# Decoder layer on one core: block sums of the down projections' weights accumulated in SBUF instead of in DRAM

## The chip, the cores and the metric

The kernel runs on one core of a Trainium2 chip. The metric is the device time of one execution in microseconds (us). TensorE (PE) does the matmuls, with its weight loads (PEld) beside them; VectorE (DVE), ScalarE (ACT) and GpSimd (POOL) work on vectors; SyncE (SP) issues most of the transfers. DMAs that GpSimd issues are on the profile's queue q0 (software_dynamic), those that SyncE issues on q1 (hardware_dynamic); both are served by the core's 16 DMA engines. A DMA that adds to its destination (`accum_op`) is issued by GpSimd here.

## The reference

One layer of a hybrid decoder on 512 tokens of width 1024, in float32:

```
def swiglu(x, w_gate, w_up, w_down):
    return (jax.nn.silu(x @ w_gate) * (x @ w_up)) @ w_down
...
        h = swiglu(rms_norm(x, ffn1_pre_norm[l]), ffn1_w_gate[l], ffn1_w_up[l], ffn1_w_down[l])
        x = x + 0.5 * rms_norm(h, ffn1_post_norm[l])
        ... # sparse attention, gated delta rule, attention to a memory of 256 rows; x = x + their gated sum
        ... # a second swiglu layer (ffn2) of the same form
```

The hidden width of both swiglu layers is 2816, that is 22 tiles of 128. The change is in the two products `@ w_down` (2816 x 1024).

## The kernel before

**Float32 as three matmuls.** Every operand x is split into hi (a cast to fp32r by ACT) and lo = x - hi (a subtraction on DVE). A product is hi\*hi + lo\*hi + hi\*lo, three matmuls. A weight tile of 128x512 (256 KB, here one *piece*) so needs a DMA into a raw tile, a cast, and a subtraction, before PE can use it.

**Seven products for eight.** Both the gate/up products (`fast_phase`) and the down projections (`down7`) use a Strassen-Winograd scheme: 2x2 blocks, seven block products of sums of blocks. In `down7` the blocks of the weights are b00, b01, b10, b11 (an index for the half of the columns, one for the half of the 22 k-tiles). Of H (the hidden activations) DVE makes the sums in SBUF (`s3`, `s2`, `s4`). Each of the seven products m0 to m6 has 11 k-tiles, two blocks of tokens and three matmuls, 66 matmuls of 128x512. The accumulators X, Y, Z, Q are pairs of PSUM banks (acc_mm, acc_e, acc_s, and acc_o with acc_r); `end...` moves or adds them into c2 (SBUF) between products. After m4 (`done(4)`) half of the tokens are complete; m5 and m6 complete the other half.

**Where the weight sums come from.** `weight_sums` writes four sums T into DRAM: t3 = b11+b01, t1 = b01+b00, t2 = t3+b00, t4 = t2+b10. It does so with DMAs on GpSimd's queue, copies first and accumulates on top (line L536). FFN1's 88 pieces of 256 KB go out during FFN1's own gate/up phase, one for each 4600 columns of matmuls (`tick`); FFN2's 32 pieces of 704 KB go out during the mixers, one for each 15000 columns. In `down7` a ring (`ringr` for raw tiles, `ringh` for hi, `lor`/`lo` for lo) then takes the pieces in pairs: load L639 on SP, cast L640, subtraction L641. Some products' tiles go through `wload` (raw tiles `wraw`, L105, L106, L109) instead.

**Around it.** The gate/up phase (f from 6 to 21) loads four quarters of 256 KB a tile f into `fq` (L413 to L416, on SP), DVE adds them into `fs` and back into `fq` (L412), ACT casts them into `fset`/`fxth` (L418, L425), DVE subtracts (L421, L426), PE multiplies (L446), ACT evicts (L452 to L461). During the down projections other transfers run too: the residual `x` (tiles xa, xb; four of 512 KB), the post gain `gb` (512 KB), and in FFN1 the memory rows `xm` (1 MB). In FFN1 the memory's norm and transposes (`mem_norm`, L208 to L213) stand between matmuls of the down projection. A tile scheduler fixes the order of instructions on each engine at build time; an instruction waits for its operands by semaphore, in that order.

Of the kernel before, what the change touches and what calls it, by code (L numbers as in the profile page):

```python
# [39 lines left out]
class Body:  # L40
    def __init__(self, ctx, tc, a, out, tap):
# [28 lines left out]
        self.own = 0  # L70
        self.side = []

# [48 lines left out]
    def tick(self, ins, cols):  # L121

        self.mmark = ins
        if self.side:
            self.cols += cols
            if self.cols >= self.pace:
                self.cols -= self.pace
                self.side.pop(0)()

# [303 lines left out]

    def fast_prods(self, S, T, banks, s7, mid=()):

        nc, v, te = self.nc, self.nc.vector, self.nc.tensor
        hi, lo = S
        a, q7, g, u = banks
        a, q7, u = a[:, :256], q7[:, :256], u[:, :256]

        def prod(out, w, t, start=False):
            th, tl = T[t]
            for k in range(4):
                c = slice(k * P, k * P + P)
                wh, wl = hi[:, w, c], lo[:, w, c]
                m = lambda x, y, **kw: te.matmul(out, x, y, skip_group_check=True, **kw)  # L446
                m(wh, th[:, k], start=start and k == 0, stop=False)
                m(wl, th[:, k], start=False, stop=False)
                self.tick(m(wh, tl[:, k], start=False, stop=k == 3), 3 * 256)
# [7 lines left out]
        nc.scalar.activation(u, a, AF.Copy, scale=-1.0)  # L457
# [66 lines left out]

    def weight_sums(self, w, n, cuts, pace):

        g = self.nc.gpsimd
        nh = self.a[w].shape[1] // 2
        T = [self.dr.tile([nh, P, 512], F32, name=f"T{n}{i}") for i in range(4)]
        v = lambda x: x.rearrange("k p n -> (k p n)").rearrange("(r c) -> r c", c=1024)  # L530
        B = lambda i, j: v(self.a[w][j, nh * i : nh * i + nh])
        t1, t2, t3, t4 = map(v, T)
        todo = ((t3, B(1, 1), 0), (t1, B(0, 1), 0), (t3, B(0, 1), 1), (t1, B(0, 0), 1), (t2, t3, 0), (t2, B(0, 0), 1), (t4, t2, 0), (t4, B(1, 0), 1))

        def piece(o, x, add, c):
            i = g.dma_start(o[c], x[c], max_dma_last_dim=2048, **({"accum_op": OP.add} if add else {}))  # L536
            self.order(i, self.mmark, mybir.DependencyClass.Sync)

        r = nh * P * 512 // 1024 // cuts
        self.pace, self.cols = pace, 0  # L540
        self.side = [lambda s=s, c=slice(r * j, r * j + r): piece(*s, c) for s in todo for j in range(cuts)]
        return T

    def down7_homes(self, n, x1, lors):
# [4 lines left out]
        self.sraw = [dw.tile([P, 4, 256], F32, name=f"sraw{i}") for i in range(2)]  # L549
        self.q7 = dw.tile([P, 2, 512], F32, name="q7")  # L550
        self.c2 = dw.tile([P, 2, 2, 512], F32, name="c2")
        lor = [dw.tile([P, 2, 512], F32R, name=f"lor{i}") for i in range(lors)]
        self.wx = None
        if lors < 4:
            self.wx = pool("wy")
            self.own = 6
        dv = pool("dv")
# [4 lines left out]
        dv = pool("dz")  # L562
        sl0, sl1, sh0, sh1 = (ch(x) for x in ("sl0", "sl1", "sh0", "sh1"))
        self.sring = [sh0, sh1, sh2, sh3], [sl0, sl1, sl2, sl3]
        return gb, lor
# [4 lines left out]

    def down7_ring(self, los):
        rings = [self.cp.tile([P, KT, SEQ], t, tag=g, name=n) for t, g, n in ((F32, "xth", "ringr"), (F32R, "xtl", "ringh"))]
        two = lambda x: [x[:, i : i + 2] for i in range(0, x.shape[1], 2)]
        self.wring = two(rings[0]), two(rings[1]), los

    def down7(self, H, w, T, banks, done, ringed, lor=()):

        nc, v = self.nc, self.nc.vector
        X, Y, Z, Q = banks
        sh, sl = self.sring  # L580
        sraw, q7, c2 = self.sraw, self.q7, self.c2
# [3 lines left out]
        tt, st = v.tensor_tensor, v.scalar_tensor_tensor  # L585

        def s3(k, n):
            t = sraw[slot % 2][:, :n]
            self.order(tt(t, h(0, 0, k, n), h(1, 0, k, n), op=OP.subtract), last)
            return t  # L590

        def s2(k, n):
            a, q = h(0, 0, k, n), h(1, 0, k, n)
            tt(q, h(1, 1, k, n), q, op=OP.subtract)
            st(a, a, -1.0, q, op0=OP.mult, op1=OP.subtract)
            return a

# [7 lines left out]

        def end7(i):
            nc.scalar.copy(q7[:, i], Q[i])

        def end6(i):
            nc.scalar.copy(Z[i], X[i])  # L610

        def end5(i):
            tt(c2[:, 1, i], Z[i], q7[:, i], op=OP.add)

        def end4(i):
            tt(c2[:, 0, i], X[i], q7[:, i], op=OP.add)

        part = lambda i, j: lambda k, n: h(i, j, k, n)
        seq = (
            (X, d[0, :nh], part(0, 0), True, end1, 0),  # L620
            (Q, T[2], s3, True, end7, 0),
            (X, T[1], s2, False, end6, 2),
            (Z, T[0], part(1, 0), False, end5, 0),
            (X, T[3], part(1, 1), False, end4, 0),
            (Y, d[0, nh:], part(0, 1), False, None, 0),
            (Z, d[1, nh:], s4, False, None, 4),
        )
        slot = wslot = 0
        last = None
        wr, wh_, wl_ = self.wring  # L630

        def weights(m, src, ks, lo):
            nonlocal wslot
            if not ringed(m, ks[0]):
                return {ks[0]: self.wload(src[ks[0]], lo=lo)}
            n, k = len(ks), ks[0]
            raw, hi, lo = wr[wslot % len(wr)][:, :n], wh_[wslot % len(wh_)][:, :n], wl_[wslot % len(wl_)][:, :n]
            wslot += 1
            nc.sync.dma_start(raw, src[k : k + n].rearrange("k p n -> p k n"))  # L639
            nc.scalar.copy(hi, raw)  # L640
            tt(lo, raw, hi.bitcast(F32), op=OP.subtract)  # L641
            return {k + i: (hi[:, i], lo[:, i]) for i in range(n)}

        for m, (acc, src, make, start, end, lag) in enumerate(seq):
            ops, ws, groups, k = {}, {}, [], 0
            while k < nh:
                n = 2 if ringed(m, k) and (nh - k) % 2 == 0 else 1
# [3 lines left out]
            lo = list(lor) if lag and not ringed(m, nh - 1) else []  # L651
            hold = len(groups) - lag
# [697 lines left out]
    def run(self):  # L1350
# [3 lines left out]
        with tc.tile_pool(name="f1", bufs=1) as fp, contextlib.ExitStack() as x1:  # L1354
# [41 lines left out]
            with tc.tile_pool(name="wx0", bufs=1) as self.wx:  # L1396
# [16 lines left out]
            with tc.tile_pool(name="st1", bufs=1) as st, tc.tile_pool(name="su1", bufs=1) as su:  # L1413
# [4 lines left out]
                self.fast_phase(1, 4, xh, xl, RB, H, step)  # L1418
                assert not self.side
            gb, lor = self.down7_homes(1, x1, 3)  # L1420
# [33 lines left out]
            uh = ul = None  # L1454
            self.down7(H, "ffn1_d", T1, banks, done, lambda m, k: m and m < 5 or not m and k > 5, [x[:, i] for x in lor for i in range(2)][:3])
        self.wx = None
        with tc.tile_pool(name="mx", bufs=1) as mp:
# [46 lines left out]
            with tc.tile_pool(name="at", bufs=1) as ap_:  # L1504
# [37 lines left out]
                with tc.tile_pool(name="at2", bufs=1) as a2:  # L1542
# [30 lines left out]
                    self.pool_every = 2  # L1573
                    T2 = self.weight_sums("ffn2_d", 2, 4, 15000)
                    self.tasks(task, PRM["order2"], "M")
                with st, tc.tile_pool(name="ms", bufs=1) as ms:
# [40 lines left out]
                    mark = E["mark"]  # L1617
                    assert not self.side
                    self.pool_every = 0
# [35 lines left out]
        with tc.tile_pool(name="f2", bufs=1) as fp, contextlib.ExitStack() as x1:  # L1655
# [29 lines left out]
            lo4 = self.cp.tile([P, 4, 512], F32R, tag="mtl", name="lo4")  # L1685
            self.down7_ring(lor + [lo4[:, :2], lo4[:, 2:]])
            pre = self.cp.tile([P, 4, 512], F32, tag="mth", name="pre")
# [14 lines left out]

            self.down7(H, "ffn2_d", T2, banks, done, lambda m, k: m or k > 5)

# [100 lines left out]
```

## Time and profile before

| | us |
|---|---|
| median of 3 runs | 1313.54 (1313.14 to 1315.1) |
| profiled execution, own time | 1313.67 |
| its span (first to last instruction) | 1311.9 |
| granted TensorE clock, mean | 0.996 |
| FFN1 gate/up phase, stretch used below | 90 to 248 |
| FFN1 down projection, m0 to m4 | 247.8 to 327.8 |
| FFN2 gate/up phase, the same work | 1046 to 1199 |
| FFN2 down projection, m0 to m4 | 1199.26 to 1274.33 |

Page rows give an engine's busy time and count. A row of the list of waits reads "who waited, at which line <- for whom: us in total, times, longest". A row by stretch of time gives its length, then each engine's busy time with its count of instructions, the granted clock (1.00 is full), the share of the DMA engines' time, and GB/s. A row of a DMA queue gives packets, MB, and the time that the packets took as a share of 16 engines over the stretch.

### The profile page before, as it was taken

What the parts mean: (1) busy time and instruction counts of PE and PEld (TensorE: products, weight loads), DVE (VectorE), ACT (ScalarE), POOL (GpSimd) and SP (SyncE); (2) the same over time, 40 slices, a digit from 0 to 9 for tenths busy, and PEclk for the clock granted to TensorE, in tenths of its full rate; (3) what the DMA queues carried; (4) which work ended last, traced back from release to release, by engine and by line L of the source; (5) the groups of instructions that cost most, each with busy time, mean ns of one, the idle gap of its engine ahead of it and who ended that gap; (6) DMA issues with size and microseconds to landing.
All of it is one profiled execution on the core that took longest, in us unless ns stands there. A gap on an engine that the chain in (4) does not pass through costs nothing. (4 is left out here: it accounts for less than half of the span.)

```text
span 1311.9 us, 21823 instructions
## 1 busy us (share of the span) xinstructions
PE 1272.6 (97%) x7959; PEld 1104.9 (84%) x7959; DVE 985.1 (75%) x1774; ACT 733.5 (56%) x1483; POOL 207.3 (16%) x233
## 2 busy tenths in 40 slices
PE   8999999999989999999999999999999999999997
PEld 7889999977878778878776778898778899999886
DVE  6898777698867866755789766564689688875986
ACT  7565556485755644415564545544577466664663
POOL 0133233100001221112221223243300000000000
PEclk9999999999999999999999999999999999999999
DMA  7779898875653342233432486577953533323764
GB/s 250 255 239 230 214 230 209 195 262 190 212 186 118 105 115 73 74 114 119 135 122 93 93 202 191 138 214 157 321 179 119 177 129 98 114 81 107 269 196 142
DMA packets 121082, 218.68 MB, mean 167 GB/s; under 512 B 19484, under 2 KB 29072, under 8 KB 120976
## 3 DMA queue, kind: packets, MB, share of 16 engines
q1 hardware_dynamic: 101872, 170.90, 40.1%
q0 software_dynamic: 18816, 46.15, 16.1%
q8 instruction: 62, 1.02, 0.3%
q14 instruction: 44, 0.36, 0.1%
q10 hardware_dynamic: 288, 0.26, 0.1%
HBM read 207.22 MB, written 56.15 MB: 201 GB/s over the span
## 5 line engine op out<-in xcount | busy, mean ns | idle before, releaser
L106 ACT CAST whi<-wraw 128x512 fp32r<-128x512 f32 (+1 forms) x226 | 136.2, 616 | 135.2 <-PE pfm L119 51.3
L109 DVE TENSOR_TENSOR wlo<-wraw,whi 128x512 fp32r<-128x512 f32 (+1 forms) x195 | 136.3, 709 | 49.5 <-ACT whi L106 48.1
L117 PE MATMUL pfm<-xth,whi 128*128 128x512 f32 x272 | 108.2, 403 | 1.0 <-DVE X L1116 0.6
L118 PE MATMUL pfm<-xth,wlo 128*128 128x512 f32 x272 | 108.2, 403 | 0.0
L119 PE MATMUL pfm<-xtl,whi 128*128 128x512 f32 x272 | 107.8, 402 | 0.0
L536 POOL DMA_DIRECT2D T<-in_ffn_d_dram x90 | 67.6, 751 | 198.8 <-PE pg L119 38.7
L640 ACT CAST ringh<-ringr 128x1024 fp32r<-128x1024 f32 (+1 forms) x66 | 63.6, 973 | 33.5 <-PE acc_mm L658 9.1
L446 PE MATMUL smm<-thi,fset 128*128 128x256 f32 x384 | 68.6, 278 | 2.8 <-ACT ss L457 2.8
L641 DVE TENSOR_TENSOR lor<-ringr,ringh 128x1024 fp32r<-128x1024 f32 (+1 forms) x54 | 59.2, 1106 | 3.2 <-ACT ringh L640 2.4
L446 PEld LDWEIGHTS smm<-thi,fset 128*128 128x128 f32 x384 | 58.2, 189 | 3.3 <-ACT ss L457 3.2
L117 PEld LDWEIGHTS pfm<-xth,whi 128*128 128x128 f32 x272 | 51.0, 188 | 11.7 <-issue 1.8
L466 DVE TENSOR_TENSOR up<-s,smm 128x256 f32<-128x256 f32 x32 | 13.5, 423 | 60.9 <-ACT se L461 60.9
L119 PEld LDWEIGHTS pfm<-xtl,whi 128*128 128x128 f32 x272 | 51.0, 189 | 9.7 <-issue 0.8
L118 PEld LDWEIGHTS pfm<-xth,wlo 128*128 128x128 f32 x272 | 50.9, 188 | 8.9
L109 POOL TENSOR_TENSOR wlo<-wraw,whi 128x512 fp32r<-128x512 f32 x28 | 38.8, 1388 | 112.5 <-ACT whi L106 98.1
L446 PE MATMUL smm<-thi,fxth 128*128 128x256 f32 x192 | 53.3, 278 | 1.3 <-ACT ss L457 1.3
L446 PE MATMUL smm<-thi,fxtl 128*128 128x256 f32 x192 | 53.3, 277 | 0.8 <-DVE fxtl L421 0.8
L446 PE MATMUL se<-thi,fset 128*128 128x256 f32 x256 | 45.2, 276 | 0.0
L1234 ACT ACTIVATE Pm<-Pm,nm 128x384 f32<-128x384 f32 (+2 forms) x64 | 35.6, 558 | 15.0 <-DVE nm L1233 14.3
L412 DVE TENSOR_TENSOR fs<-fq 128x1024 f32<-128x1024 f32 x32 | 39.1, 1221 | 6.5 <-issue 3.9
L671 DVE TENSOR_TENSOR sl<-H,sh 128x1024 fp32r<-128x1024 f32 (+2 forms) x38 | 41.1, 1083 | 3.7 <-ACT sh L670 3.7
L658 PE MATMUL acc_mm<-ringh,sl 128*128 128x512 f32 x108 | 42.0, 389 | 0.0
(622 smaller groups left out, 4293.2 us busy)
## 6 DMA issues: line engine op xcount, KB each, us to landing
ringr<-T SPq DMA_DIRECT2D x40, 512.0 KB, 4.7
T<-in_ffn_d_dram POOLq DMA_DIRECT2D x66, 256.0 KB, 5.8
T<-in_ffn_d_dram POOLq DMA_DIRECT2D x24, 704.0 KB, 7.4
fq<-in_ffn_g_dram SPq DMA_DIRECT2D x64, 256.0 KB, 3.6
fq<-in_ffn_u_dram SPq DMA_DIRECT2D x64, 256.0 KB, 3.9
wraw<-in_ffn_g_dram SPq DMA_DIRECT2D x34, 256.0 KB, 3.5
wraw<-in_ffn_u_dram SPq DMA_DIRECT2D x34, 256.0 KB, 3.6
wraw<-in_ffn_d_dram SPq DMA_DIRECT2D x34, 256.0 KB, 3.6
```

The source lines that it names most:

```text
L106: nc.scalar.copy(hi, raw)
L109: eng.tensor_tensor(lo, raw, hi.bitcast(F32), op=OP.subtract)
L117: t.matmul(out, lh, rh, start=first, stop=False)
L118: t.matmul(out, ll, rh, start=False, stop=False)
L119: self.tick(t.matmul(out, lh, rl, start=False, stop=last), 3 * math.prod(out.shape[1:]))
L412: add = lambda *x: v.tensor_tensor(*x, op=OP.add)
L446: m = lambda x, y, **kw: te.matmul(out, x, y, skip_group_check=True, **kw)
L536: i = g.dma_start(o[c], x[c], max_dma_last_dim=2048, **({"accum_op": OP.add} if add else {}))
L640: nc.scalar.copy(hi, raw)
L641: tt(lo, raw, hi.bitcast(F32), op=OP.subtract)
L658: e = lambda a, b, s, f: nc.tensor.matmul(acc[i], a, b, start=s, stop=f, skip_group_check=True)
L671: last = tt(low, f, hi.bitcast(F32), op=OP.subtract)
```

## The change

The sums are no longer kept in DRAM: `weight_sums` and `tick` are gone. The order of the seven products and the sums of H are changed so that the weight operand of each of m1, m2, m3 is the one before it plus one block: m0 uses b00, m1 b00+b01, m2 adds b11, m3 adds b10. The raw tile of each k stays in SBUF over m0 to m3. After DVE has subtracted it (L635), a DMA on GpSimd's queue adds the next block onto the same raw tile (L633, `accum_op`), and the result is cast (L634) and subtracted again. m4 uses b11+b01: SP loads b11 into the raw tile, then GpSimd's queue adds b01. m5 and m6 use b10 and b11 alone. A down projection so has 44 accumulated pieces (256 KB each). Because raw tiles have homes of their own, FFN1 uses 9 groups of tiles a product (seven singles, two pairs) and FFN2 8 groups (five singles, three pairs), where the ring had 6 (one single, five pairs). The sums of H are s1, s2, s3, s4 now, each formed in one product. At the ends of products, a block of tokens had three ACT copies and two DVE additions; now it has four and three. The number of PE instructions is the same, 7959.

```diff
-        self.tick(t.matmul(out, lh, rl, start=False, stop=last), 3 * math.prod(out.shape[1:]))
+        self.mmark = t.matmul(out, lh, rl, start=False, stop=last)
...
+    def down7_ring(self, los, ext=None):
+        raw, hi = [self.cp.tile([P, KT, SEQ], t, tag=g, name=n) for t, g, n in ((F32, "xth", "ringr"), (F32R, "xtl", "ringh"))]
+        at = [(ext, 2), (ext, 0), (ext, 1)] if ext is not None else []
+        self.wring = at + [(raw, i) for i in range(KT)], [hi[:, i : i + 2] for i in range(0, KT, 2)], los
...
+        def s1(k, n):
+            q = h(1, 0, k, n)
+            self.order(tt(q, h(1, 1, k, n), q, op=OP.subtract), last)
+            return q
...
         seq = (
-            (X, d[0, :nh], part(0, 0), True, end1, 0),
-            (Q, T[2], s3, True, end7, 0),
-            (X, T[1], s2, False, end6, 2),
-            (Z, T[0], part(1, 0), False, end5, 0),
-            (X, T[3], part(1, 1), False, end4, 0),
-            (Y, d[0, nh:], part(0, 1), False, None, 0),
-            (Z, d[1, nh:], s4, False, None, 4),
+            (X, part(0, 0), (b00,), True, end1, 0),
+            (Z, s1, (None, b01), True, end5, 0),
+            (X, s2, (None, b11), False, end6, 2),
+            (X, part(1, 1), (None, b10), False, end4, 0),
+            (Q, s3, (b11, b01), True, end7, 0),
+            (Y, part(0, 1), (b10,), False, None, 0),
+            (Z, s4, (b11,), False, None, 4),
         )
...
+            if not m and k < early:
+                wp, bufs = (self.wp, self.WB) if k < self.WB[0] else (self.wx, self.WX)
+                one = lambda i, t, g: wp.tile([P, 512], t, tag=g, name=g, bufs=bufs[i]).rearrange("p (o n) -> p o n", o=1)
+                keep[k] = raw = one(0, F32, "wraw")
+                hi, lo = one(1, F32R, "whi"), one(2, F32R, "wlo")
+            else:
+                hi, lo = wh_[wslot % len(wh_)][:, :n], wl_[wslot % len(wl_)][:, :n]
+                wslot += 1
+                if k < early:
+                    raw = keep[k]
+                else:
+                    t, o = homes[k - early]
+                    raw = t[:, o : o + n]
+            for i, x in enumerate(src):
+                if x is not None:
+                    e, add = (nc.gpsimd, {"accum_op": OP.add}) if i else (nc.sync, {})
+                    e.dma_start(raw, x[k : k + n].rearrange("k p n -> p k n"), **add)
             nc.scalar.copy(hi, raw)
             tt(lo, raw, hi.bitcast(F32), op=OP.subtract)
...
-                T1 = self.weight_sums("ffn1_d", 1, 11, 4600)
...
-                    T2 = self.weight_sums("ffn2_d", 2, 4, 15000)
```

How the order of instructions changes on POOL in FFN1's gate/up phase and down projection (T_717 is t3, T_715 t1, T_716 t2, T_718 t4; sg is the gate activation). Before:

```order
L536 DMA T_715<-in_ffn_d_dram 128x512 x8
L536 DMA T_717<-in_ffn_d_dram 128x512 x11
L536 DMA T_715<-in_ffn_d_dram 128x512 x11
L536 DMA T_716<-T_717 128x512 x11
L536 DMA T_716<-in_ffn_d_dram 128x512 x11
L536 DMA T_718<-T_716 128x512 x11
L536 DMA T_718<-in_ffn_d_dram 128x512 x11
```

After:

```order
L307 TENSOR_TENSOR sg<-sg,RB 128x256 x3
L633 DMA wraw<-in_ffn_d_dram 128x512 x5
L633 DMA ringr<-in_ffn_d_dram 128x512
L633 DMA wraw<-in_ffn_d_dram 128x512
L633 DMA ringr<-in_ffn_d_dram 128x2x512 x2
L633 DMA wraw<-in_ffn_d_dram 128x512 x6
```

The 88 issues of the gate/up phase are gone, and the accumulates of m1, m2, ... stand on the queue one product after another, each of them waiting for DVE's subtraction of the same raw tile in the product before.

SP in FFN1's down projection (xm are the memory rows, xb and xa the residual). Before, from m2 (T_716) to m4 (T_718):

```order
L639 DMA ringr<-T_716 128x2x512 x5
L715 DMA xm<-in_mem_dram 128x2x1024
L639 DMA ringr<-T_715 128x512
L639 DMA ringr<-T_715 128x2x512 x2
L105 DMA wraw<-in_ffn_d_dram 128x512
L639 DMA ringr<-T_715 128x2x512 x2
L105 DMA wraw<-in_ffn_d_dram 128x512 x3
L706 DMA gb<-in_ffn_post_dram 128x1024
L691 DMA xb<-in_x_dram 128x1024 x2
L639 DMA ringr<-T_715 128x2x512
L639 DMA ringr<-T_718 128x512
```

After, from m0's last loads to m4:

```order
L633 DMA wraw<-in_ffn_d_dram 128x512 x2
L633 DMA ringr<-in_ffn_d_dram 128x512
L633 DMA ringr<-in_ffn_d_dram 128x2x512 x2
L709 DMA xm<-in_mem_dram 128x2x1024
L633 DMA wraw<-in_ffn_d_dram 128x512
L700 DMA gb<-in_ffn_post_dram 128x1024
L685 DMA xb<-in_x_dram 128x1024
L685 DMA xa<-in_x_dram 128x1024 x2
L685 DMA xb<-in_x_dram 128x1024
L633 DMA wraw<-in_ffn_d_dram 128x512 x5
L633 DMA ringr<-in_ffn_d_dram 128x512
L633 DMA ringr<-in_ffn_d_dram 128x2x512 x2
```

SP has no loads for m1, m2 and m3 any more; the memory rows, the gain and the residual follow right behind m0's loads, and ten of m4's eleven pieces stand behind them. In FFN2 all of m0's ring loads, then the four residual loads, two of m4's pieces, the gain, and the rest of m4's come in that order.

More of the change, by code (lines that the diff above doesn't have):

```diff
@@ L448, in prod @@
                 m(wl, th[:, k], start=False, stop=False)
-                self.tick(m(wh, tl[:, k], start=False, stop=k == 3), 3 * 256)
+                self.mmark = m(wh, tl[:, k], start=False, stop=k == 3)
         prod(a, self.S_A11, self.T_B11, True)
@@ L523, in down_half @@
                 mm(i, k)
[L525 to L542, printed above, removed]
     def down7_homes(self, n, x1, lors):
@@ L563, in down7_homes @@
         sl0, sl1, sh0, sh1 = (ch(x) for x in ("sl0", "sl1", "sh0", "sh1"))
+        if lors == 4:
+            self.ext = dv.tile([P, 3, 512], F32, name="rawx")
         self.sring = [sh0, sh1, sh2, sh3], [sl0, sl1, sl2, sl3]
@@ L569, in down7_banks, with down7 @@
         return b4[:2], c4[:2], c4[2:], b4[2:]
[L571 to L576, printed above, removed]
+    def down7_ring(self, los, ext=None):
+        raw, hi = [self.cp.tile([P, KT, SEQ], t, tag=g, name=n) for t, g, n in ((F32, "xth", "ringr"), (F32R, "xtl", "ringh"))]
+        at = [(ext, 2), (ext, 0), (ext, 1)] if ext is not None else []
+        self.wring = at + [(raw, i) for i in range(KT)], [hi[:, i : i + 2] for i in range(0, KT, 2)], los
+    def down7(self, H, w, banks, done, ringed, lor=()):
         nc, v = self.nc, self.nc.vector
@@ L585, in down7, with s2 @@
         tt, st = v.tensor_tensor, v.scalar_tensor_tensor
+        def s1(k, n):
+            q = h(1, 0, k, n)
+            self.order(tt(q, h(1, 1, k, n), q, op=OP.subtract), last)
+            return q
+        def s2(k, n):
+            a = h(0, 0, k, n)
+            st(a, a, -1.0, h(1, 0, k, n), op0=OP.mult, op1=OP.subtract)
+            return a
         def s3(k, n):
             t = sraw[slot % 2][:, :n]
-            self.order(tt(t, h(0, 0, k, n), h(1, 0, k, n), op=OP.subtract), last)
+            self.order(st(t, h(0, 0, k, n), -1.0, h(1, 1, k, n), op0=OP.mult, op1=OP.subtract), last)
             return t
[L592 to L596, printed above, removed]
         def s4(k, n):
@@ L604, in end1, with end5, end4, end6 @@
             nc.scalar.copy(Y[i], X[i])
-        def end7(i):
[L607 to L616, printed above, removed]
+        def end5(i):
+            nc.scalar.copy(c2[:, 1, i], Z[i])
+        def end4(i):
+            nc.scalar.copy(c2[:, 0, i], X[i])
+        def end6(i):
+            tt(c2[:, 1, i], c2[:, 1, i], X[i], op=OP.add)
+            nc.scalar.copy(Z[i], c2[:, 1, i])
+        def end7(i):
+            for h in range(2):
+                tt(c2[:, h, i], c2[:, h, i], Q[i], op=OP.add)
         part = lambda i, j: lambda k, n: h(i, j, k, n)
+        b00, b10, b01, b11 = [d[i, nh * j : nh * j + nh] for i in range(2) for j in range(2)]
         seq = (
-            (X, d[0, :nh], part(0, 0), True, end1, 0),
-            (Q, T[2], s3, True, end7, 0),
-            (X, T[1], s2, False, end6, 2),
-            (Z, T[0], part(1, 0), False, end5, 0),
-            (X, T[3], part(1, 1), False, end4, 0),
-            (Y, d[0, nh:], part(0, 1), False, None, 0),
-            (Z, d[1, nh:], s4, False, None, 4),
+            (X, part(0, 0), (b00,), True, end1, 0),
[5 more added lines that the diff above has]
+            (Z, s4, (b11,), False, None, 4),
         )
@@ L629, in down7 @@
         last = None
-        wr, wh_, wl_ = self.wring
+        homes, wh_, wl_ = self.wring
+        early = nh - (5 if self.wx else 7)
+        keep = {}
         def weights(m, src, ks, lo):
             nonlocal wslot
-            if not ringed(m, ks[0]):
-                return {ks[0]: self.wload(src[ks[0]], lo=lo)}
             n, k = len(ks), ks[0]
-            raw, hi, lo = wr[wslot % len(wr)][:, :n], wh_[wslot % len(wh_)][:, :n], wl_[wslot % len(wl_)][:, :n]
-            wslot += 1
-            nc.sync.dma_start(raw, src[k : k + n].rearrange("k p n -> p k n"))
+            if not ringed(m):
+                return {k: self.wload(src[0][k], lo=lo)}
+            if not m and k < early:
[15 more added lines that the diff above has]
+                    e.dma_start(raw, x[k : k + n].rearrange("k p n -> p k n"), **add)
             nc.scalar.copy(hi, raw)
@@ L642, in weights @@
             return {k + i: (hi[:, i], lo[:, i]) for i in range(n)}
-        for m, (acc, src, make, start, end, lag) in enumerate(seq):
+        for m, (acc, make, src, start, end, lag) in enumerate(seq):
             ops, ws, groups, k = {}, {}, [], 0
             while k < nh:
-                n = 2 if ringed(m, k) and (nh - k) % 2 == 0 else 1
+                n = 2 if ringed(m) and k >= early and (nh - k) % 2 == 0 else 1
                 groups.append(list(range(k, k + n)))
@@ L650, in down7 @@
             cuts = (0, 1, 4, 8, nh) if m == 0 else (0, 4, 8, nh)
-            lo = list(lor) if lag and not ringed(m, nh - 1) else []
+            lo = list(lor) if lag and not ringed(m) else []
             hold = len(groups) - lag
@@ L1418, in run @@
                 self.fast_phase(1, 4, xh, xl, RB, H, step)
-                assert not self.side
             gb, lor = self.down7_homes(1, x1, 3)
@@ L1454, in run @@
             uh = ul = None
-            self.down7(H, "ffn1_d", T1, banks, done, lambda m, k: m and m < 5 or not m and k > 5, [x[:, i] for x in lor for i in range(2)][:3])
+            self.down7(H, "ffn1_d", banks, done, lambda m: m < 5, [x[:, i] for x in lor for i in range(2)][:3])
         self.wx = None
@@ L1617, in run @@
                     mark = E["mark"]
-                    assert not self.side
                     self.pool_every = 0
@@ L1685, in run @@
             lo4 = self.cp.tile([P, 4, 512], F32R, tag="mtl", name="lo4")
-            self.down7_ring(lor + [lo4[:, :2], lo4[:, 2:]])
+            self.down7_ring(lor + [lo4[:, :2], lo4[:, 2:]], self.ext)
             pre = self.cp.tile([P, 4, 512], F32, tag="mth", name="pre")
```

14 lines of the change are left out of this document (2 added, 12 removed).

## The prediction

> **What bounds the kernel now.** I read the page first (span, engines, queues), then PE's waits by stage, then the DMA queues in the stages that the change touches.
>
> ```profile
> span 1311.9 us, 21823 instructions
> PE 1272.6 (97%) x7959; PEld 1104.9 (84%) x7959; DVE 985.1 (75%) x1774; ACT 733.5 (56%) x1483; POOL 207.3 (16%) x233
> q1 hardware_dynamic: 101872, 170.90, 40.1%
> q0 software_dynamic: 18816, 46.15, 16.1%
> ```
>
> PE is busy 97% of the span, and its instructions stay the same. So the change can only gain where PE waits now, and loses wherever it makes PE wait. The DMA engines are far from full on average (40.1% and 16.1%), but the average hides two stages. FFN1's gate phase runs beside the sums' DMAs, FFN2's does not, and both do the same work:
>
> ```profile
> 90.00:248.00 158.00, 153.41 (x1319) 152.51 (x1319) 115.49 (x137) 88.33 (x182) 50.21 (x71) 0.99 0.89 209
> 1046.00:1199.00 153.00, 152.74 (x1339) 152.54 (x1338) 115.91 (x138) 90.40 (x186) 0.00 (x0) 1.00 0.29 91
> PE smm L446 <- ACT ss L457: 4.1, 4, 2.1
> PE smm L446 <- DVE fxtl L421: 0.5, 1, 0.5
> ...
> PE smm L446 <- DVE fxtl L421: 0.3, 1, 0.3
> ```
>
> The first two waits are FFN1's stretch (90 to 248), the last is the only one from FFN2's gate phase to the end. DMA share is 0.89 against 0.29. The largest FFN1 wait leads back to a transfer:
>
> ```profile
> 152.62 1.23 DVE L412 TENSOR_TENSOR fs<-fq 128x1024 f32<-128x1024 f32 x1 [2.61 <-issue]
> 153.88 0.62 ACT L425 CAST fset<-fs 128x512 fp32r<-128x512 f32 x1 [2.94 <-DVE fs L412]
> 154.82 0.50 PE L446 MATMUL smm<-thi,fset 128*128 128x256 f32 x2 [2.12 <-ACT ss L457]
> 155.00:157.00 2.00, 2.00 (x14) 2.00 (x15) 0.58 (x1) 1.14 (x2) 0.52 (x1) 0.69 0.64 186
> 157.00:160.00 3.00, 3.00 (x19) 3.00 (x19) 2.07 (x3) 1.43 (x3) 0.27 (x1) 0.64 0.57 193
> DMA to landing us min/median/max: 3.1/5.4/8.1
> ```
>
> DVE stood 2.61 us before it could add a quarter `fq` whose DMA was late (landings of `fq` take 3.1 to 8.1 us here, last row), ACT's cast and eviction came after it, PE waited 2.12 us, and then the granted clock was 0.69 and 0.64 over the next 5 us.
>
> The other stage is the down projections. In FFN2's:
>
> ```profile
> 1199.26 15.12 PE acc_mm L658 x66
> ...
> 1259.37 14.96 PE acc_mm L658 x66
> 1274.33 14.96 PE acc_e L658 x66
> 1229.00:1244.00 15.00, 15.00 (x68) 12.43 (x67) 15.00 (x16) 10.97 (x14) 0.00 (x0) 1.00 0.94 339
> 247.80:327.80 80.00, 77.45 (x348) 63.40 (x347) 72.65 (x91) 55.52 (x75) 0.00 (x0) 1.00 0.69 237
> ```
>
> PE goes through product after product at 15.0 us each with no wait; m0 to m4 end 75.1 us after the start. In FFN1 the same five take 80.0 us (last row), with the memory's transposes and waits in it. Here the change puts 44 accumulating pieces a projection in place of plain loads.
>
> **The price of an accumulated piece.** No row shows an accumulate into SBUF. The nearest are those into DRAM:
>
> ```profile
> q0 software_dynamic: 1506, 4.95, 32.5%
> q0 software_dynamic: 2827, 5.17, 71.7%
> q1 hardware_dynamic: 2455, 4.47, 31.1%
> q0 software_dynamic: 1354, 2.48, 90.5%
> q1 hardware_dynamic: 2118, 4.71, 88.2%
> T<-in_ffn_d_dram POOLq DMA_DIRECT2D x21, 256.0 KB, 6.9
> ```
>
> Row 1 is q0 from 52 to 98 us, where the sums are plain copies: 46 x 0.325 / 4.95 = 3.02 us of all 16 engines per MB. Rows 2 and 3 are 104 to 148 us, where q0 carries only accumulates (last row, 21 of them): 44 x 0.717 / 5.17 = 6.10 us per MB, beside plain loads at 44 x 0.311 / 4.47 = 3.06. So the same queue's accumulate costs twice its copy. A piece is 0.262 MB: 1.60 and 0.80 us; since the two shares sum to 1.03 I scale both, to 1.55 and 0.78. Row 4 (224 to 244 us, accumulates alone) gives 20 x 0.905 / 2.48 = 7.3, 1.91 us a piece: the high end. Row 5 (1235 to 1250 us, plain loads alone) gives 15 x 0.882 / 4.71 = 2.81, 0.74 us a piece: the low end, if adding in SBUF cost no more than writing. I take 1.55, from the row nearest in kind (accumulates beside loads); that the destination is SBUF may cheapen it, and I hold that against the dearer row 4.
>
> The Trainium skill's page "DMA: Bandwidth & Descriptors", section "Anatomy of one DMA — SWDGE (gpsimd) path", fits a DMA issued from GpSimd as about 2.0 us fixed plus bytes at 436 GB/s. By it a piece would hold the engines an estimated 0.60 us, accumulate or not, and the sum below would come to no stall at all. This trace disagrees: 1.55 for accumulates, 0.74 for the best plain loads.
>
> **The change part by part.**
>
> *Sums in the gate phase go (gain).* FFN1's waits fall from 4.6 us to about FFN2's 0.3, and the slow clock goes: about 5 us at 0.66 cost 1.7. Together 4.3 + 1.7 = 6.0 us less. Next in line there is `fxtl`'s 0.3, as in FFN2. FFN2's sums run beside the mixers, where I credit nothing: PE's waits there are on vector work.
>
> *FFN2's accumulates (loss).* m4's last pair must land before its cast, subtraction and matmuls:
>
> ```profile
> L640 ACT CAST ringh<-ringr x66: 607/1052/1059, 251.5 to 1293.2; 128x1024 fp32r<-128x1024 f32 x54, 128x512 fp32r<-128x512 f32 x12
> L641 DVE TENSOR_TENSOR lor<-ringr,ringh x54: 683/1223/1239, 253.0 to 1294.3; 128x1024 fp32r<-128x1024 f32 x42, 128x512 fp32r<-128x512 f32 x12
> L671 DVE TENSOR_TENSOR sl<-H,sh x38: 426/1217/1237, 247.6 to 1289.1; 128x1024 fp32r<-128x1024 f32 x22, 128x768 fp32r<-128x768 f32 x14, 128x256 fp32r<-128x256 f32 x2
> L536 POOL DMA_DIRECT2D T<-in_ffn_d_dram x90: 523/812/987, 54.0 to 920.5; - x90
> ```
>
> The pair's matmuls take 2/11 of 15.0 = 2.7 us, the cast 1.05, the subtraction 1.22, so it must land by 75.1 - 5.0 = 70.0 us after the start. Until then the engines carry: m0's pieces 4 to 10, 7 x 0.78 = 5.5; the residual, 8 pieces' worth, 6.2; the gain, 2 pieces, 1.6; 41 accumulates (three of the 44 are released early, as m0's first tiles are prepared in the gate phase) x 1.55 = 63.6; m4's plain loads, 11 x 0.78 = 8.6. That is 85.5, and 1.3 for the first to be subtracted and issued: 86.8. Stall: 16.8 us. It assumes that the engines never idle, which is kind: each accumulate waits for a subtraction.
>
> *FFN1's (loss).* The same, and the memory rows, 4 pieces, 3.1: 89.9, against 80.0 - 5.0 = 75.0. Stall: 14.9 us.
>
> *Issue and order.* An accumulate costs POOL about 0.81 us to issue (row above; 36 issues in FFN1, 32 in FFN2, 29 and 26 us of POOL in 80, on an engine that is idle there). Behind a waiting accumulate on POOL stand only the next ones. On SP in FFN1 the gain, the residual and the rest of m4's loads queue behind m4's first piece, which waits for m3's subtraction; the residual is wanted after m4, so only m4's loads count, above.
>
> *Latency alone.* Round one raw tile: subtraction 0.69 of a single, issue 0.81, landing 5.3 in the median and 10.7 at worst (into T), cast 0.61, subtraction 0.69:
>
> ```profile
> DMA to landing us min/median/max: 2.5/5.3/10.7
> DMA to landing us min/median/max: 2.5/4.5/8.7
> ```
>
> That is 8 to 13.5 us, under the 15.0 of a product, and for m4, with a load of 4.5 more (second row, `ringr`), about 13. So latency without queueing costs nothing; its cover is a lead of less than 2 us at worst.
>
> *Groups and sums on DVE and ACT.* Two more singles-for-pairs a product in FFN2 (2 x (2 x 0.69 - 1.22), 0.3 us of DVE) and three in FFN1 (0.5). s2's two steps go from one product to two, which takes DVE below the 15.00 of 15 that it shows in the window from 1229. m4 gets s3 and additions. Its eight groups are 5 x 0.69 + 3 x 1.22 = 7.1 us; s3 and the split `sl` each pass over 11 x 256 columns, at 1.22 for 1024 (row above) 3.4; an addition of 512 is like a single, 2 x 0.69: in all 15.3 us, 0.3 over the product, but m4 then waits for its transfers anyway. I put these at 0; between -1 and +3, since FFN1 has only three `lo` pairs.
>
> The sum: 16.8 + 14.9 - 6.0 = +25.7 on the profiled execution's 1313.67 (its span is 1311.9; the median of the runs, 1313.54, is 0.13 lower): 1339.
>
> With c the price of an accumulate, the two stalls are 41(c - 1.14) + 41(c - 1.19). Below c = 1.14 there is none. They pay back the gate phase's 6.0 at c = 1.24.
>
> **The rivals.**
>
> *B, other side: accumulates at a plain load's price.* At 0.74 to 0.78 a piece FFN2 needs 23.2 + 41 x 0.78 = 55.2 us of 70; everything hides, and the gate phase's 6.0 remain: 1308, down to 1307 with DVE's relief. For it: T is in DRAM, the raw tiles are not, and reading the destination may be the dear part. Against: copies from DRAM to DRAM cost no more than loads (3.02 against 3.06), so where the bytes lie has moved nothing so far, and the doubling came with the adding. It decides below c = 1.24. The skill's fit, above, is this rival by rule.
>
> *C: dearer, as from 224 to 244.* c = 1.91: stalls 31.6 + 29.5, less 6.0, +55: 1369. For it: that stretch had no loads beside it, and each accumulate there also had a freshly written source. Against: the last passes read from in_ffn_d_dram as the earlier ones did.
>
> *D: engines idle between accumulates.* At c about 1.3, each group's wait for its subtraction leaves gaps, and PE's stall delays the next subtraction. That reaches the forecast's size by another road, 1325 to 1340; every wait over 2 us that halves the clock as at 155 adds 1.7.
>
> *E: c near 1.24,* gain and loss cancel: 1311 to 1316.
>
> **How the numbers follow.** Forecast A with D (c from 1.3 to 1.75): 0.65, 1318 to 1356. C: 0.13. E: 0.05. B: 0.17. What a measurement can tell here is about 0.2%, 2.6 us. Faster takes B, 0.16; same E and B's edge, 0.06; slower the rest, 0.78. The range goes from E's upper half, 1315, to C's 1370.
>
> **What would show it.** Right: no PE wait over 0.5 us from 90 to 240 and clock 1.00 there, DMA share about 0.3 as in FFN2's gate phase; in both down projections a DMA share of 0.9 and more with q0 near 6 us per MB, accumulates' landings growing from m1 to m4, PE waiting at m3 and m4 on ACT's cast or DVE's subtraction, which wait for DMAs, and m5 and m6 again at 15.0. Wrong: q0 near 3 us per MB in the down projections (B); landings short but POOL waiting long for DVE (D); or a DMA share under 0.8 while PE stalls, which no term above has.

## The result, and the profile after

The changed kernel takes 1328.07 us (median of 4, 1325.86 to 1332.07), the kernel before on the same chip 1314.28. The ratio is 1.0109, with an interval of 1.0081 to 1.0137. 1339 was forecast, with a range of 1315 to 1370. The profiled execution took 1329.57 us. From its page, the span, the first row of part 1, and q1 and q0 of part 3:

```profile
span 1327.8 us, 21815 instructions
PE 1280.4 (96%) x7959; PEld 1107.7 (83%) x7959; DVE 981.8 (74%) x1801; ACT 738.3 (56%) x1510; POOL 190.9 (14%) x181
q1 hardware_dynamic: 92976, 153.59, 35.8%
q0 software_dynamic: 12352, 23.07, 9.8%
```

Half of q0's bytes are gone (46.15 MB before), and on average the DMA engines are less busy. The span is 15.9 us longer all the same. Its stages, from the first and last matmuls of each in the two traces:

| stage | before | after | change | forecast |
|---|---|---|---|---|
| FFN1 gate phase | 177.6 | 170.3 | -7.3 | -6.0 |
| FFN1 down, m0 to m4 | 80.0 | 91.4 | +11.4 | +14.9 |
| FFN1 down, m5, m6 | 38.5 | 42.5 | +4.0 | 0 |
| between the layers (mixers) | 678.8 | 673.8 | -5.0 | 0 |
| FFN2 gate phase | 153.9 | 154.5 | +0.6 | 0 |
| FFN2 down, m0 to m4 | 75.1 | 84.9 | +9.9 | +16.8 |
| FFN2 down, m5, m6 | 30.1 | 32.1 | +2.0 | 0 |
| all else | 77.8 | 78.1 | +0.3 | 0 |

By stretch of time, after: the two gate phases, then FFN2's m1 and m2 (1219 to 1249), m3 (1249 to 1269) and m4 (1269 to 1289):

```profile
90.00:245.00 155.00, 154.51 (x1336) 153.62 (x1336) 118.37 (x142) 92.42 (x188) 0.85 (x1) 1.00 0.31 97
1048.80:1203.30 154.50, 153.85 (x1345) 153.44 (x1343) 116.41 (x137) 91.12 (x187) 0.95 (x2) 1.00 0.31 94
1219.00:1249.00 30.00, 30.00 (x134) 24.83 (x133) 26.42 (x29) 20.12 (x28) 15.94 (x16) 1.00 1.13 207
1249.00:1269.00 20.00, 16.66 (x65) 12.98 (x64) 15.81 (x20) 9.68 (x13) 5.58 (x6) 0.91 1.07 266
1269.00:1289.00 20.00, 18.10 (x72) 14.15 (x71) 10.00 (x12) 9.68 (x13) 2.40 (x2) 0.91 0.95 248
```

FFN1's gate phase now reads like FFN2's: DMA share 0.31 for 0.89, PE busy 154.5 of 155, clock 1.00. In FFN2's down projection the DMA share is over 1 from m1 to m3 (the times of packets on one engine overlap), and from m3 on PE is no longer busy throughout and the granted clock is 0.91. m2 and m3 together took 35.4 us there and m4 19.0, for 30.0 and 15.0 before, so the loss is not m4's alone. PE's waits, in FFN1's m0 to m4 (240 to 333 us; first three rows) and in FFN2's (1203 to 1290 us; the rest):

```profile
PE acc_o L652 <- ACT ringh L634: 5.9, 3, 3.3
PE acc_s L652 <- ACT sh L664: 1.9, 1, 1.9
PE acc_o L652 <- DVE lor L635: 1.1, 2, 0.5
...
PE acc_mm L652 <- DVE lor L635: 2.6, 1, 2.6
PE acc_o L652 <- ACT ringh L634: 1.4, 1, 1.4
PE acc_mm L652 <- DVE c L588: 0.7, 1, 0.7
```

acc_o is m4's accumulator, acc_mm in FFN2's rows that of m2 and m3, and the waits lead to the cast and the subtraction of weights, as forecast. But they sum to only 8.9 us in FFN1 (2.6 before), and 5.6 in FFN2 with two small ones not shown, where the stages grew by 11.4 and 9.9.

### The profile page after: what moved, and what is told of

It reads as the page before. It is cut to its first block, busy times and chain, and to the rows that moved or that the text cites. A ratio compares the mean times of both kernels' runs of the same rounds, so it can differ in the third digit from the quotient of the medians.

```text
span 1327.8 us, 21815 instructions
## 1 busy us (share of the span) xinstructions
PE 1280.4 (96%) x7959; PEld 1107.7 (83%) x7959; DVE 981.8 (74%) x1801; ACT 738.3 (56%) x1510; POOL 190.9 (14%) x181
## 5 line engine op out<-in xcount | busy, mean ns | idle before, releaser
L105 ACT CAST whi<-wraw 128x512 fp32r<-128x512 f32 (+1 forms) x214 | 128.3, 615 | 135.1 <-PE pfm L118 63.2
L108 DVE TENSOR_TENSOR wlo<-wraw,whi 128x512 fp32r<-128x512 f32 (+1 forms) x183 | 125.1, 693 | 48.1 <-ACT whi L105 46.8
L633 POOL DMA_DIRECT2D wraw<-in_ffn_d_dram x40 | 35.6, 961 | 459.6 <-DVE wlo L635 395.6
L652 PE MATMUL acc_mm<-ringh,sh 128*128 128x512 f32 x112 | 44.9, 401 | 0.7 <-DVE c L588 0.7
L652 PE MATMUL acc_mm<-ringh,sl 128*128 128x512 f32 x112 | 45.1, 402 | 0.0
L634 ACT CAST ringh<-wraw 128x512 fp32r<-128x512 f32 x48 | 29.6, 619 | 25.5 <-DMA wraw<-in_ffn_d_dram 10.3
L652 PE MATMUL acc_mm<-lor,sh 128*128 128x512 f32 x102 | 41.2, 404 | 2.6 <-DVE lor L635 2.6
```

What stands on the lines that cost most here:

```text
L108: eng.tensor_tensor(lo, raw, hi.bitcast(F32), op=OP.subtract)
L633: e.dma_start(raw, x[k : k + n].rearrange("k p n -> p k n"), **add)
L652: e = lambda a, b, s, f: nc.tensor.matmul(acc[i], a, b, start=s, stop=f, skip_group_check=True)
```

## What an accumulate cost

The DMA queues in 1219 to 1249 us of the changed kernel, where q0 has the engines nearly to itself, and a row of its issues; the last row is SP's queue in 300 to 307 us, where it has the engines to itself with plain loads:

```profile
q0 software_dynamic: 3243, 6.09, 111.7%
q1 hardware_dynamic: 39, 0.08, 0.8%
ringr<-in_ffn_d_dram POOLq DMA_DIRECT2D x4, 512.0 KB, 9.8
...
q1 hardware_dynamic: 1328, 2.81, 102.8%
```

6.09 MB in 30 us is 203 GB/s: 1.29 us for a piece of 0.262 MB. The forecast took 1.55 from accumulates into DRAM. The share of 111.7% also shows why a share is a poor price where engines are full: 30 x 1.117 / 6.09 would give 1.44 us. Plain loads by the same measure, 2.81 MB in 7 us, run at 401 GB/s: 0.65 us a piece, where the forecast took 0.78. With c = 1.29 the prediction's formula gives stalls of 41 x 0.15 + 41 x 0.10 = 10.3 us, less than half of the 21.3 measured to the ends of m4. With 0.65 for its 28 and 32 plain pieces as well, 3.6 and 4.2 us more go, and 2.5 us are left in FFN2 and nothing in FFN1. The experiments look for the rest.

## Experiments

**1. The sums left out of the kernel before.**

```diff
-        T = [self.dr.tile([nh, P, 512], F32, name=f"T{n}{i}") for i in range(4)]
...
+        return [self.a[w][j, nh * i : nh * i + nh] for i, j in ((1, 1), (0, 1), (0, 0), (1, 0))]
```

> The kernel before, with none of the DMAs that make the weight sums; the four products that read a sum read one block of the weights from DRAM in its place, by the same loads. It so leaves the summing out. Theory (the sums' transfers delay the loads of FFN1's gate phase and of the mixers): about 1301, that is 7.3 us less in FFN1's gate phase and 5.0 us less between the two feed-forward layers, as the changed kernel shows, and nothing in the down projections. Rival (those stages gained by the new order of instructions, not by the missing transfers): 1311 to 1314.

Measured: 1305.38 us where the kernel before took 1314.58, ratio 0.9928 (0.9902 to 0.9955). In the profile FFN1's gate phase is 170.3 us (177.6 before) and the mixers 670.7 (678.8). Both stages gain with nothing else changed, so the sums' transfers cost them their time; the gain of 9.2 us is 3 short of the 12.3 expected from the stages, and FFN1's down projection, where nothing was expected, is 121.3 us in this profile (118.6). Experiments 5 and 6 assign the two. The gain of the gate phase differs from profile to profile: the five that have the sums beside it show 173.4 to 178.5 us, eight of the nine without them 170.3 (the ninth is in the last section), so it is 3 to 8 us.

**2. The accumulates as plain loads.**

```diff
-                    e, add = (nc.gpsimd, {"accum_op": OP.add}) if i else (nc.sync, {})
+                    e, add = (nc.gpsimd if i else nc.sync), {}
```

> The changed kernel, with the 88 accumulating pieces as plain loads on the same queue, in the same order and with the same waits; it so leaves the adding out. Theory (an accumulate holds the DMA engines 1.28 us a piece where a load holds them 0.65, and that is the down projections' loss): no stall of the two projections over 2 us, no halved clock there, 1300 to 1306. Rival (the loop subtraction, issue on POOL, landing, cast costs it, whatever the transfer does): the down projections stay 20 us or more longer, 1320 to 1328. Second rival (more groups on DVE and ACT): they stay 5 to 15 us longer with the waits on DVE, 1308 to 1318.

Measured: 1310.72 us, ratio 0.9969 (0.9946 to 0.9993), against 1.0109 with the accumulates: the theory's direction, 4.7 us above its upper end. The queues in 1214 to 1244 us, and PE's waits there (FFN2, 1198 to 1312 us) and in FFN1 (240 to 333 us):

```profile
q0 software_dynamic: 1768, 6.12, 61.0%
...
PE acc_mm L652 <- ACT sh L664: 0.4, 1, 0.4
...
PE acc_o L652 <- ACT ringh L634: 2.4, 1, 2.4
PE acc_s L652 <- ACT sh L664: 1.8, 1, 1.8
PE acc_o L652 <- DVE lor L635: 0.4, 1, 0.4
```

The same bytes on the same queue hold the engines 61% instead of 112%, and all of FFN2's waits go but 0.4 us: its down projection takes 105.7 us (105.15 before, 117.0 changed). The loop of subtraction, issue and landing costs FFN2 nothing by itself. FFN1 keeps 125.4 us (118.6 before): 6.8 of its 15.4 us are not the adding's by these profiles, and 4 to 7 if the old order's spread in six profiles, 118.0 to 121.3, is allowed for. They lie at the start of m1, which waits for ACT's cast of s1 (`sh`), in m4, and in m5 and m6 (41.7 us for 38.5); no experiment separates what of the new order causes them.

**3. Another order of the last three products.**

```diff
+            seq = seq[:4] + (
+                (Z, s4b, (b11,), False, None, 0),
+                (Q, s3b, (None, b01), True, end7, 0),
+                (Y, part(0, 1), (b10,), False, None, 4),
+            )
```

> The changed kernel with its last three products in another order in both projections: b11 alone (with s4, written into a buffer of its own) comes right after m3, then b01 is added onto that same raw tile (with s3), then b10. So m4's extra plain load of b11 is gone (11 pieces a projection), and the last accumulates have one product more of time; half of the tokens end one product later. Theory (transfers are the bound in m0 to m4): with 1.28 and 0.65 us a piece the engines need about 72 us by a deadline of 85 and about 50 us for m3 by one of 55, so there is no stall, and 1302 to 1309. Rival (the loop of subtraction, issue and landing bounds each product): 1320 or more. Rival (the later ends lengthen the tail and the start of the mixers): 1308 to 1316, with the loss behind the last product.

Measured: 1331.92 us, ratio 1.0131 (1.01 to 1.0162). The expectation failed. The projections did get shorter (124.2 us for 133.9, 111.0 for 117.0), though FFN2's m3 kept a wait of 2.5 us. That wait is the changed kernel's (below, 4): DVE stood 3.8 us for the gain. And the mixers grew from 673.8 to 686.3 us, about 5 us of it by their middle and 6.7 around the start of FFN2, the tail from 7.4 to 10.1, and FFN2's gate phase ran at its slower pace (last section), 159.4 us for 154.5. The order helps the transfers and harms what comes behind; around the start of FFN2 PE stood 3.3 us for one cast of a gate weight, and the granted clock was 0.57 from 988 to 996 us after it; why that cast was late was not traced.

**4. The residual and the gain behind m4's loads.**

```diff
-                if m == 1:
-                    x.extend(self.load_x(dx2, after=self.mmark))
-                if m == 2:
+                if m == 3:
                     self.gain7("ffn2_post", 0.5 * self.RK, gb)
                 if m == 4:
+                    x.extend(self.load_x(dx2, after=self.mmark))
```

(and the same in FFN1)

> The changed kernel, with the residual x and the post gain loaded later in both projections (on SP they stand behind m4's loads). Nothing is left out. Theory (the transfers before m4's deadline are the bound): 10 pieces' worth of plain loads at about 0.65 us leave each window, so each projection's stall at m4 shrinks by 5 to 6.5 us and the halved clock goes with it where the wait falls under 2 us: 1313 to 1320. Rival (waits in the loop subtraction, issue, landing): 1326 to 1330, no change. Rival (the residual is now late for the ends of m4 and delays the mixers' first transposes): 1322 to 1330, with new waits behind m4.

Measured: 1325.77 us, ratio 1.0075 (1.0042 to 1.0108). FFN1's down projection fell from 133.9 to 125.8 us. Why is seen in the changed kernel's timeline of POOL and PE, at m4's first accumulates, and in SP's own waits (284 to 306 us):

```profile
304.43 0.86 POOL L633 DMA_DIRECT2D wraw<-in_ffn_d_dram  x1 [10.57 <-DMA wraw<-in_ffn_d_dram]
311.85 0.50 PE L652 MATMUL acc_o<-ringh,sh 128*128 128x512 f32 x1 [3.34 <-ACT ringh L634]
...
SPq L685 <- PE ptr L198: 4.7, 1, 4.7
```

POOL stood 10.57 us for one of m4's plain loads, which had the residual in front of it on SP's queue and in the engines. SP itself had stood 4.7 us at the residual's load (L685), for the memory's transposes: xm and xa share a buffer. Almost no accumulate ran meanwhile: in 300 to 307 us q0 moved 0.02 MB. FFN2, however, kept its stall (85.8 us to the end of m4). The timeline of this run, DVE and PE:

```profile
1274.13 0.76 DVE L703 TENSOR_SCALAR gb<-gb 128x512 f32<-128x512 f32 x2 [8.88 <-DMA gb<-in_ffn_post_dram]
1274.81 1.22 DVE L635 TENSOR_TENSOR lor<-rawx,ringh 128x1024 fp32r<-128x1024 f32 x1
1276.08 0.80 PE L652 MATMUL acc_o<-lor,sh 128*128 128x512 f32 x1 [6.90 <-DVE lor L635]
```

DVE's queue is in order. The gain's scaling stood at its head for 8.88 us, since the gain's transfer was slow among accumulates; m4's subtraction was behind it, and PE behind that. The changed kernel itself has the same thing at m3:

```profile
1257.06 0.76 DVE L703 TENSOR_SCALAR gb<-gb 128x512 f32<-128x512 f32 x2 [3.80 <-DMA gb<-in_ffn_post_dram]
1257.74 1.82 DVE L635 TENSOR_TENSOR lor<-rawx,ringh 128x512 fp32r<-128x512 f32 x2
1258.48 0.50 PE L652 MATMUL acc_mm<-lor,sh 128*128 128x512 f32 x1 [2.60 <-DVE lor L635]
```

So the list of waits named DVE's subtraction, and the wait was for a transfer of 512 KB that nobody needed yet.

**5 and 6. The change in one layer alone.** Each kernel has the old `down7` and `weight_sums` for the other layer.

```diff
-            self.down7(H, "ffn2_d", banks, done, lambda m: True)
+            self.old7(H, "ffn2_d", T2, banks, done, lambda m, k: m or k > 5)
```

> The changed kernel's down projection and its dropped sums in FFN1 alone; FFN2 has the sums in DRAM, made in the mixers, and the projection of the kernel before. By the stages of the two profiles: 1314.4 - 7.3 (gate phase) + 15.4 (down projection) = 1322; if the 5.0 us between the two layers were FFN1's doing, 1317.

> The changed kernel's down projection and its dropped sums in FFN2 alone; FFN1 has the sums in DRAM, made in its gate phase, and the projection of the kernel before. By the stages of the two profiles: 1314.4 - 5.0 (mixers) + 11.9 (down projection) + 0.4 = 1322; if the 5.0 us were not FFN2's sums but a side effect of FFN1, 1326.

Measured: 1326.6 us (ratio 1.0083, 1.0052 to 1.0113) and 1324.77 us (1.0073, 1.0045 to 1.0101), the kernel before 1316.27 beside them. Both layers lose alone, by 10.3 and 8.5 us, more than the 8 and 8 expected. FFN1's gate phase is 170.3 us in the first and 178.5 in the second; the mixers are 679.6 and 673.1 us. So the 7.3 us hang on FFN1's sums and the 5 us on FFN2's, each as assumed. In both profiles FFN2's gate phase ran at its slower pace (last section), which the expectations did not reckon with; how much of the 2 us too many that makes is not known.

**7. FFN2 alone, with the other order and the late residual.**

> As the one with the change in FFN2 alone, with the last three products of FFN2 in the other order (b11 alone, then b01 added onto it, then b10) and the residual and gain loaded behind m4's loads. Theory (transfers): by m3's deadline of 55 us the engines carry about 4.6 + 38.4 + 1.3 = 44 us, by that of the last accumulates, 85, about 65, so no stall is left in FFN2; 5.0 less in the mixers and up to 3 more behind the last product, as the run with the other order in both showed: 1310 to 1314. Rival (the wait of about 2.5 us at m3 that the other order left is the loop's latency, and not the residual's transfers): it stays, 1315 to 1320.

The edit joins those of 3 and 4, in FFN2. Measured: 1316.19 us, ratio 0.9985 (0.9959 to 1.0012): no difference from the kernel before, 2.2 us above the expected stretch. All of PE's waits from 1196 us to the end of FFN2's matmuls:

```profile
PE acc_e L835 <- DVE lo L818: 1.9, 1, 1.9
PE acc_mm L835 <- ACT sh L847: 0.4, 1, 0.4
```

With 44 accumulates still there, m0 to m4 take 75.5 us, as with the sums in DRAM, and m3's wait of experiment 3 is gone, since the gain's transfer, with no residual ahead of it, now lands before DVE asks for it. So it was not the loop's latency. What is left is in the last product (DVE busy with the ends) and a tail of 9.3 us.

**8. The gain early.**

```diff
-                if m == 2:
+                if m == 0:
                     self.gain7("ffn2_post", 0.5 * self.RK, gb)
```

> The changed kernel, with FFN2's post gain loaded ahead of the residual (asked for after m0 and not after m2); nothing is left out. In the profile of the changed kernel DVE stands 3.80 us before the gain's scaling, with subtractions of m3's weights behind it, PE waits 2.60 us for one of them, and its clock is halved after it. Theory (DVE's queue blocked by the gain's late transfer is a part of FFN2's loss): that wait goes, m0 to m4 of FFN2 end at 78 to 81 us after the start and not at 84.95, 1322 to 1325. Rival (the transfers are late anyway, and only the name of the wait changes): 84 to 86 us, 1327 to 1330.

Measured: 1325.05 us, ratio 1.0082 (1.0061 to 1.0103), at the upper end. DVE's wait for the gain is gone, but m0 to m4 of FFN2 still take 83.4 us: m3's 2.6 us went, and the waits for `c` (1.8 us for 0.7) and for `ringh` in m4 (2.1 for 1.4) grew. The rival's "only the name of the wait changes" is nearer here. With the residual still in front, m4's pieces are late anyway.

**9. The ends of experiment 7 turned round.**

```diff
-        for h in range(2):
+        for h in hs:
...
-                        self.ending([banks[1][i], banks[2][i]], x, gb, i, self.out, tmp)
+                        self.ending([banks[1][i], banks[2][i]], x, gb, i, self.out, tmp, (1, 0))
```

> As the run with FFN2's products in the other order and the residual late, and FFN1 as before; but the last ends take the half that is complete after m4 (Z) first, and the half of the last product (Y) last. Its tail behind the last product was 9.27 us where the kernel before has 7.64, since both halves' ends stood behind the last product. Theory: 7.4 to 7.7 us of tail, 1.6 to 2 less than that run: 1313 to 1315 where the kernel before takes 1316, ratio 0.997 to 0.999. Rival (the earlier ends take DVE's time from the last product's weights): no gain, PE waits over 2 us in the last product.

Measured: 1309.54 us, with 1313.4 before, ratio 0.9975 (0.9959 to 0.9991). It beats the changed kernel, and the kernel before by a quarter of a per cent, which is clear of the noise. The tail fell to 8.4 us, not to 7.5.

**10. Residual late and gain early, both layers, the changed kernel's own order.**

> The changed kernel in its own order of products, with the residual behind m4's loads and the gain ahead of everything but m0's, in both projections; nothing is left out. With the residual late, FFN2 had kept its stall (85.8 us to the end of m4), since DVE then stood 8.88 us before the gain's scaling, m4's last subtractions behind it. Theory (FFN2's loss is the transfers in front of m4's and DVE's queue behind the gain, together): with both gone the five products of FFN2 take 76 to 80 us and those of FFN1 85 to 87, 1313 to 1320. Rival (the accumulates alone are too much for m4): FFN2 82 us or more, 1322 to 1327.

Measured: 1317.59 us, ratio 1.0037 (1.001 to 1.0063). FFN2's m0 to m4 take 79.7 us, FFN1's 86.7: both in the expected stretches. Neither edit did it alone in FFN2; together they give back more than half of what its m0 to m4 had lost. What is left there, 4.6 us, stands in m4, which takes 19.2. (In FFN1 the late residual alone had given 86.9.) PE's waits in FFN2 (1195 to 1318 us), the two longest:

```profile
PE acc_e L652 <- DVE lor L635: 2.3, 1, 2.3
PE acc_o L652 <- ACT ringh L634: 1.3, 2, 1.2
```

The 2.3 us now stand in m5, where four additions and the ends of m4 are ahead on DVE.

**11 and 12. Both kernels once more.**

> The kernel before, once more with a profile. In the earlier profiles FFN2's gate phase took 153.9 to 154.5 us for three kernels and 158.8 to 159.4 us for six, by matmuls at 0.113 or 0.118 us, with no waits. If that is a state of the execution, this profile may show 159 us; if it hangs on the kernel, 153.9 again.

> The changed kernel, once more with a profile. FFN2's gate phase: 154.5 us again if the pace of its matmuls hangs on the kernel, and 159 us possible if it is a state of the execution. The stalls of the down projections within 2 us of the first profile (91.4 and 84.95 us for m0 to m4).

1310.82 and 1328.13 us, one run each. FFN2's gate phase: 153.94 and 154.53 us, as the first time. The stalls repeated (89.4 us in FFN1, 84.5 in FFN2).

## Why the prediction was right, and where it was not

**Forecast A held:** slower, because accumulates fill the DMA engines and m4's weights come late. Taking the adding away takes the loss away in FFN2 (experiment 2), and less traffic ahead of m4 shrinks it (4 with 10, 7). Of its signs, FFN1's gate phase came as written; q0 took 4.9 us per MB and not 6, and m5 and m6 did not come back to 15.0. That the number fell into the range is in part luck: several terms were off, and made up for one another.

**The gate phase** was sized well: 6.0 forecast, 7.3 measured, and by the reason given (experiments 1 and 5). The row with 2.61 us had no releaser ("issue"); that a late transfer was behind it is shown by experiment 1, not by that row.

**The mixers** were the term left out: "where I credit nothing: PE's waits there are on vector work" was read from the engines' names. In the kernel before, PE's waits from 780 to 900 us, and DVE shortly before:

```profile
PE pfm L117 <- DVE tg L1315: 1.3, 1, 1.3
PE de L446 <- DVE mset L421: 0.8, 1, 0.8
...
876.99 1.23 DVE L412 TENSOR_TENSOR msum<-mfq 128x1024 f32<-128x1024 f32 x1 [2.37 <-DMA mfq<-in_w_gate_dram]
```

The mixers' own gate weights came late beside the sums' 704 KB pieces, as `fq` did in FFN1. After the change one wait of 0.2 us is left in that stretch, and the stage is 5.0 us shorter. These waits make 2.7 us with one of 0.6 not shown; where PE lost the other 2.3 was not traced, but the whole 5 go with the sums (experiments 1, 5 and 6).

**The prices** were mis-sized: an accumulate at 1.55 us, by the row of accumulates into DRAM, for 1.29 into SBUF, and a plain load at 0.78 for 0.65. The first by itself would have brought the sum to 10.3 - 6.0 = +4.3, that is 1318, the low end of forecast A; both together to 2.5 - 6.0 = -3.5, that is 1310, a kernel a little faster than before. So the prediction's list of transfers, rightly priced, does not give the loss.

**What the list left out** is seen in the queues from FFN2's start to the end of its last accumulate (1203.3 to 1282.5 us), and in SP's and POOL's timelines:

```profile
q0 software_dynamic: 5712, 10.75, 74.3%
q1 hardware_dynamic: 4158, 9.10, 33.6%
...
1262.46 8.34 SPq L633 DMA_DIRECT2D wraw<-in_ffn_d_dram  x4
1273.04 6.16 SPq L633 DMA_DIRECT2D rawx<-in_ffn_d_dram  x2
...
1272.25 1.19 POOL L633 DMA_DIRECT2D ringr<-in_ffn_d_dram  x1 [1.01 <-DMA ringr<-in_ffn_d_dram]
```

10.75 MB are the 41 accumulates that were counted; 9.10 MB are 34.7 plain pieces where the sum has 28 (FFN1, 241 to 327.1 us: 10.39 MB, 39.6 for 32). The others are m5's: SP issues seven of its pieces (the SP rows) before m4's last pair of accumulates has landed. At 203 and 401 GB/s an estimated 53 + 23 = 76 of the 79.2 us are transfer time. The last pair so lands 9.2 us after the 70.0 that the prediction asked for, and the stage grew by 9.9: that the transfers decide when m4 ends fits. The engines' idle time, the assumption that the text called "kind", is about 3.5 us of it. D's reason for idling, waits for subtractions, is not what m1 and m2 show (q0 ran at 203 GB/s from 1219 to 1249 us). No run holds m5's loads back, so what they cost alone is not measured.

Seen from PE, the rest of the 21.3 us is made of three parts, which overlap with that account. PE's clock halves after some of its waits:

```profile
1256.00:1263.00 7.00, 4.52 (x13) 3.58 (x14) 5.94 (x8) 2.61 (x3) 1.72 (x2) 0.76 1.04 245
1276.00:1283.00 7.00, 5.10 (x14) 3.57 (x14) 2.45 (x2) 2.20 (x3) 0.00 (x0) 0.76 1.05 247
```

7 us at 0.76 cost 1.7 each, as after 155 us in the kernel before. A wait of 2.60 us was enough (first row), and in m4 one of 1.4 with one of 0.5 behind it; but one of 2.38 us in FFN1's m4 left the clock at 1.00 (324.8 to 331.8 us), so the length of a wait alone does not decide it. The Trainium skill's page "TensorE: Matmul & The Clock Gate", in its Part 1, has the half clock come after an idle window of about 3.4 us; no wait here was that long in FFN2, so the measurement decides. In FFN2 the two stretches make 3.4 us (they are the stretches at 0.91 above); FFN1 has two more, 249 to 256 us at 0.76 and 309 to 320 at 0.84, another 3.4. A second part is what stands at the head of a queue: the residual ahead of m4's loads on SP, with POOL behind them (10.57 us), and the gain on DVE. The prediction said of SP's order that "only m4's loads count", and so counted the residual's bytes but not what waited behind them. Of DVE it named no queue at all: the gain's scaling, with subtractions behind it, was never on the list. The third is what stays of FFN1's m0 to m4 without the adding: 83.7 us in experiment 2, for 80.0 in the kernel before (79.5 to 82.8 over the six profiles of the old order).

**Groups and sums** were put at 0, "between -1 and +3". In m5 and m6 the lists show it wrong: FFN2 grew by 2.0 us there and FFN1 by 4.0; experiment 10 shows the wait in FFN2, behind m4's additions and ends on DVE.

So errors went against each other: dear prices and a missing gain (mixers) made the forecast too high; m5's loads, queue heads and the clock, which its sum left out, made it too low. **B** fell as a price: an accumulate took 1.29 us, a plain load on the same queue 0.78 (experiment 2, 61.0% for 6.12 MB). Its limit of 1.24 was not the test, though: with plain loads at 0.65 the formula balances at 1.33, and 1.29 would have given 1310, between **B** and **E**. **C**, 1.91, fell too. The Trainium skill's fit for a DMA issued from GpSimd (page "DMA: Bandwidth & Descriptors", section "Anatomy of one DMA — SWDGE (gpsimd) path"), an estimated 0.60 us of engine time a piece, is not what the accumulates show.

## What to carry to other kernels

An accumulating DMA is no free sum: into SBUF it took 1.29 us for 256 KB where plain loads on SP's queue took 0.65 with the engines full, so budget the engines stage by stage, not by the average share, and count the loads of the next stage that are issued early. When transfers get slower, look at the head of every in-order queue: an early load that nobody needs yet, or a small vector operation that waits for it, then holds up the work behind it. The list of waits names the last link (DVE's subtraction); the timeline one step further back names the transfer.

## What was not expected of the hardware

The matmuls of a gate phase ran at one of two paces with the granted clock at 1.00 and no waits. From 1060 to 1150 us, in the kernel before (profiled again) and in experiment 9:

```profile
1060.00:1150.00 90.00, 90.00 (x791) 90.00 (x790) 73.18 (x86) 55.14 (x112) 0.00 (x0) 1.00 0.34 108
...
1060.00:1150.00 90.00, 90.00 (x766) 90.00 (x765) 70.48 (x82) 54.40 (x110) 0.00 (x0) 1.00 0.34 108
```

791 matmuls against 766 in 90 us: 0.114 and 0.117 us each, 153.9 to 154.5 or 158.8 to 159.4 us for the phase. Of the fourteen profiles seven had the fast pace in FFN2 and seven the slow one. The changed kernel (twice fast) and experiment 2 (slow) have the same list of PE instructions with the same waits, so it isn't that list; experiments 1 and 2 ran on one chip, 8 and 9 on another, and each pair has a fast and a slow profile, so it isn't the chip; in experiment 10 it was FFN1's gate phase that took 175.2 us, where the others without sums there took 170.3. What sets it stays open. It is up to 5.5 us, so stages were compared here and not only totals.
